# A SwiGLU FFN's first pair of column blocks by plain products in token halves instead of seven products, and its operand sums in place, on one Trainium2 core

## Chip, cores and metric

The kernel runs on one core of a Trainium2 chip. The metric is the device time of one execution in microseconds, lower is better.

## The reference

One layer over 1024 tokens of width 1024, all in float32. What matters here is its second half:

```python
x = layer_norm(DEEPNORM_ALPHA * x + mix, ln1_g[l], ln1_b[l])      # mix: attention branches, gated, projected
gu = x @ w_ffn_in[l]                       # 1024 x 1024 by 1024 x 5632
g, u = jnp.split(gu, 2, axis=-1)           # 2816 columns each
ffn = (jax.nn.silu(g) * u) @ w_ffn_out[l]
x = layer_norm(DEEPNORM_ALPHA * x + ffn, ln2_g[l], ln2_b[l])
```

Ahead of it stand the input projection, two attention branches of eight heads each, their gates and the output projection `mix`.

## The kernel before

Every float32 operand is split in a high part (rounded, written by ScalarE's copy, L109) and a low part (the rest, by VectorE's subtraction, L110), and a product is three matmuls: high by high, high by low, low by high.

The FFN's up stage works on 22 pairs `f`: one block of 128 gate columns (the left weights, `wL`) and one of 128 up columns (the right weights, `wR`). A pair is a 2 by 2 block product: rows are the two halves of the tokens (LO: 0 to 511, HI: 512 to 1023, in the kernel's order), columns are gate and up, and the inner dimension is cut in two halves of four k-tiles. It is computed with seven block products P1 to P7 instead of eight, in the order of `pair_steps`: P1, P2, P6, P5, P7, P3, P4. Each product (`product`, L171) has 4 k-tiles x 3 = 12 matmuls of 128x128 by 128x512, so a pair has 84. P1 goes to the accumulator `sx`, P2 to `sy`, P6 and P7 and P4 add on to `sx`, P5 goes to `sz` and P3 adds to it. Between them ScalarE and VectorE move partial results to SBUF (L188, L184, L197, L201), apply Silu to the gate (L850, L855) and multiply by up (L852, L856).

The weights' sums for a pair are made by `prep_right` (four subtractions of 512 columns and two splits of 1024), a split by `prep_left` and one by `prep_last`. The sums of the tokens' operands are made once, by `x1_operands`, from the first LayerNorm's output: after four token tiles (`hf` 0) TensorE transposes them (L789), and x1A1 (the operands of P1 and P2) is split from PSUM, with a plain copy `x1raw`; after the last four (`hf` 1) the other half is transposed, and for each of four k-tiles one after the other VectorE and ScalarE make `s13` (L803 to L805), x1A22 (P4's operand, L807), `s24` (L809, L810), and the splits x1S63 (P6 and P3) and x1S57 (P5 and P7). P1 and P2 thus need only the first four token tiles, all others need the last.

The output projection before it (`half_k` 1) goes through eight token tiles: 24 matmuls of the projection, VectorE's addition (L912), and the LayerNorm (L764 to L776; for the last two tiles of each half the end is VectorE's L771). The weights of pairs 0 to 2 are loaded and prepared around that loop.

`run_pairs` sets the order of the text: P1 and P2 of the first three pairs (`first=3`), then the rest of pair 0, the right weights of pair 1 after its first product, and so on. The order in which each engine's queue gets its instructions isn't that of the text: a scheduler at build time simulates the kernel and takes, for each engine, the first instruction in the text whose inputs and slots it believes ready. On the chip each queue is then worked in that fixed order. In the trace transposes (L789) stand between the matmuls of P1 and P2 (L171), for instance.

SBUF is handed out in slots of 128 x 1024 by tag (bw 9, pt 4, yt 3, gt 3, kp 4, op 8, xt 16, and the four tags of `QKV` with 2 each); PSUM in banks: mm 2, sc 2, tr 3, pv 1. A new tile waits until a slot of its tag is free. P1's accumulator takes "mm" (pair 2: "pv"), P2's and P5's "sc".

Of the kernel before, what the change touches and what calls it, by code (L numbers as in the profile page):

```python
# [12 lines left out]
F32R = mybir.dt.float32r  # L13
AF = mybir.ActivationFunctionType
ALU = mybir.AluOpType
# [32 lines left out]
def hybrid_trunk_kernel(ctx: ExitStack, tc, x, xt, w_in, b_gate, rel_bias, w_proj,  # L48
# [14 lines left out]
    def slot(tag, name, dtype=F32):  # L63
        return pool.tile([P, 1024], dtype, tag=tag, name=name, bufs=SLOTS[tag])
# [3 lines left out]
    def cycle(tags, name, dtype=F32):  # L68

        turn_of[tags] = turn_of.get(tags, -1) + 1  # L70
        return slot(tags[turn_of[tags] % len(tags)], name, dtype)
# [3 lines left out]
    def bank(tag, name):  # L75
        return ps.tile([P, HW], F32, tag=tag, name=name, bufs=BANKS[tag])
# [31 lines left out]
    def split(dst_h, dst_l, src):  # L108
        nc.scalar.copy(dst_h, src)  # L109
        nc.vector.tensor_tensor(dst_l, src, dst_h.bitcast(F32), ALU.subtract)  # L110

    def mm3(acc, pairs):
        n = len(pairs)
        i = 0
        for lh, ll, rh, rl in pairs:
            mm(acc, lh, rh, start=(i == 0), stop=False)  # L116
            mm(acc, lh, rl, start=False, stop=False)  # L117
            i += 1
            mm(acc, ll, rh, start=False, stop=(i == n))  # L119
# [8 lines left out]
    def prep_left(W, nm, src, tag="op"):  # L128
        L = W["L"] = slot("gt", f"wL{nm}")
        dma(L, src)  # L130
        W["hl"] = split_w(L, f"wl{nm}", tag)

    def split_w(raw, nm, tag):
        h = slot(tag, f"{nm}h", F32R)
        l = slot(tag, f"{nm}l", F32R)
        split(h, l, raw)
        return h, l

    def prep_right(W, nm, src, tag, tag_a=None):
        sub = ALU.subtract  # L140
        L = W["L"]
        R = W["R"] = slot("gt", f"wR{nm}")
        dma(R, src)
        ta = slot("kp", f"ta{nm}")
        tb = slot("kp", f"tb{nm}")
        nc.vector.tensor_tensor(ta[:, LO], R[:, LO], L[:, LO], sub)
        nc.vector.tensor_tensor(tb[:, LO], R[:, HI], ta[:, LO], sub)
        nc.vector.tensor_tensor(tb[:, HI], L[:, HI], tb[:, LO], sub)
        W["hb"] = split_w(tb, f"wb{nm}", tag)
        nc.vector.tensor_tensor(ta[:, HI], R[:, HI], R[:, LO], sub)  # L150
        W["ha"] = split_w(ta, f"wa{nm}", tag_a or tag)

    def prep_last(W, nm, tag):

        c = slot(tag, f"wc{nm}", F32R)
        split(c[:, LO], c[:, HI], W["R"][:, HI])
        W["c"] = c
# [216 lines left out]

        return pair_steps(f"p{i}", Wa[i], ops_x, c, done)

    def run_pairs(steps, left, right, also=lambda i: None, first=2, aside=lambda i: None):

        n = len(steps)
        for j in range(first):  # L380
            steps[j][0]()
            steps[j][1]()
        for i in range(n):
            rest = steps[i][2:] if i < first else steps[i]
            for j, p in enumerate(rest):
                p()
                if j == 0 and i + 1 < n:
                    right(i + 1)
                if j == 1 and i + 2 < n:
                    left(i + 2)  # L390
                aside(i)
            also(i)
# [384 lines left out]
            done(slice(0, D))  # L777

    ops_1 = {p: [] for p in range(1, 8)}
    x1raw = []  # L780

    def x1_operands(hf, acc_t):

        for kt in range(4):
            tps = []
            for k in (kt, kt + 4):
                tp = bank("tr", f"x1ps{hf}_{k}")
                for j in range(4):
                    tr(tp[:, j * P:(j + 1) * P], acc_t[4 * hf + j][:, k * P:(k + 1) * P], ident)  # L789
                tps.append(tp)  # L790
            if hf == 0:
                raw = slot("op", f"x1raw{kt}")
                for i in range(2):
                    o = slot("xt", f"x1A1{i}_{kt}", F32R)
                    split(o[:, LO], o[:, HI], tps[i])
                    nc.scalar.copy(raw[:, (LO, HI)[i]], tps[i])
                    ops_1[1 + i].append((o[:, LO], o[:, HI]))
                x1raw.append(raw)
            else:
                raw = x1raw[kt]  # L800
                s13 = slot("kp", f"x1s13_{kt}")
                s24 = slot("kp", f"x1s24_{kt}")
                nc.scalar.copy(s13[:, LO], tps[1])  # L803
                nc.vector.tensor_tensor(s13[:, HI], raw[:, LO], tps[0], ALU.subtract)
                nc.vector.tensor_tensor(s13[:, LO], tps[0], s13[:, LO], ALU.add)  # L805
                o = slot("bw", f"x1A22_{kt}", F32R)
                split(o[:, LO], o[:, HI], tps[1])  # L807
                ops_1[4].append((o[:, LO], o[:, HI]))
                nc.vector.tensor_tensor(s24[:, LO], s13[:, LO], raw[:, LO], ALU.subtract)  # L809
                nc.vector.tensor_tensor(s24[:, HI], raw[:, HI], s24[:, LO], ALU.subtract)  # L810
                for src, pa, pb, tags in ((s24, 6, 3, ("xt",)), (s13, 5, 7, QKV)):
                    h = cycle(tags, f"x1S{pa}{pb}h_{kt}", F32R)
                    l = cycle(tags, f"x1S{pa}{pb}l_{kt}", F32R)
                    split(h, l, src)
                    ops_1[pa].append((h[:, LO], l[:, LO]))
                    ops_1[pb].append((h[:, HI], l[:, HI]))

    for tt in range(8):
        dma(acc_t[tt], x[tt * P:(tt + 1) * P, :])
# [3 lines left out]

    Wf = [dict() for _ in range(NF)]
    def left_f(f):
        prep_left(Wf[f], f"f{f}", w_ffn_in[f], "pt" if f == 2 else "op")

    def right_f(f):
        prep_right(Wf[f], f"f{f}", w_ffn_in[NF + f], ("bw", "pt")[f % 2],
                   "op" if f == 1 else None)  # L830
        if f:
            prep_last(Wf[f], f"f{f}", "op")

    def up_steps(f):

        tl = {}

        def c(name):

            if name == "12":  # L840
                if "h" not in tl:
                    tl["h"] = cycle(("yt", "yt", "yt", "bw"), f"h{f}")
                return tl["h"][:, LO]
            if "t" not in tl:
                tl["t"] = slot(("yt", "yt", "bw")[f] if f < 3 else "kp", f"gt{f}")
            return tl["t"][:, LO if name == "11" else HI]

        def done(name, acc):
            if name == "11":
                nc.scalar.activation(c("11"), c("11"), AF.Silu)  # L850
            elif name == "12":
                nc.vector.tensor_tensor(c("12"), c("12"), c("11"), ALU.mult)  # L852
            elif name == "21":
                h = tl["h"]
                nc.scalar.activation(h[:, HI], acc, AF.Silu)  # L855
                nc.vector.tensor_tensor(h[:, HI], h[:, HI], c("22"), ALU.mult)  # L856
                if f in pair_of:
                    h_tiles[f] = h
                    if f % 2:
                        pieces.extend(left_sums(f - 1))  # L860
                else:
                    dma(h_dr[f], h)

        return pair_steps(f"f{f}", Wf[f], ops_1, c, done, "pv" if f == 2 else "mm")
# [34 lines left out]
    for half_k in range(2):  # L899
        wo = [load_w(w_out[(4 * half_k + j) * P:(4 * half_k + j + 1) * P, :], f"o{half_k}_{j}",  # L900
                     of("gt"), of("xt"), nc.vector) for j in range(4)]
        if half_k == 1:
            left_f(0)
            right_f(0)
            left_f(1)
        for tt in range(8):
            ts_ = slice(tt * P, (tt + 1) * P)
            for hf, cs in enumerate((LO, HI)):
                acc = bank("mm" if hf == 0 else "sc", f"ops{half_k}_{tt}_{hf}")
                mm3(acc, [(mh[4 * half_k + j][:, ts_], ml[4 * half_k + j][:, ts_],  # L910
                           wo[j][0][:, cs], wo[j][1][:, cs]) for j in range(4)])
                nc.vector.scalar_tensor_tensor(  # L912
                    acc_t[tt][:, cs], acc_t[tt][:, cs], ALPHA if half_k == 0 else 1.0, acc,
                    ALU.mult, ALU.add)
            if half_k == 1:
                layer_norm(acc_t[tt], g1, b1, f"1_{tt}", tt % 4 >= 2)
                dma(x1_dr[tt], acc_t[tt])
                if tt % 4 == 3:
                    x1_operands(tt // 4, acc_t)
                if tt == 3:  # L920
                    left_f(2)

    prep_last(Wf[0], "f0", "op")
    run_pairs([up_steps(f) for f in range(NF)], lambda f: left_f(f) if f > 2 else None, right_f,
              first=3, aside=next_piece)


    acc_t = [slot("op", f"x1_{tt}") for tt in range(8)]
# [154 lines left out]
```

## Time and profile before

| | us |
|---|---|
| median of 3 runs | 1477.51 (1477.05 to 1479.56) |
| the profiled execution's own time | 1477.29 |
| its span, first to last instruction | 1475.2 |
| TensorE (PE) busy | 1431.1 |
| VectorE (DVE) busy | 1040.6 |
| ScalarE (ACT) busy | 678.4 |
| GpSimd (POOL) busy | 279.6 |

In lines of the profile, `PE` is TensorE's matmuls and `PEld` its weight loads, which run beside them. `L171` is line 171 of the kernel. A timeline line has the start, the busy time, engine, line, operation, `output<-inputs` by the program's names without their numbers at the end, shapes and count; in brackets the idle time before it and what ended that. A line of waits has the waiting engine, line and tile, what it waited for, the total, the number of waits and the longest. Matmuls overlap in such lines: each shows 0.39 us, but the next starts before it ends.

### The profile page before, as it was taken

To read this page: it belongs to the slowest core of one execution; us is meant where nothing else is said; L and a number is where in the kernel's file an instruction comes from. 1 tells how busy PE (TensorE), PEld (TensorE's weight loads), DVE (VectorE), ACT (ScalarE), POOL (GpSimd) and SP (SyncE) were. 2 spreads that over 40 slices of the span, in tenths; PEclk is the share of its full clock that TensorE was granted. 3 is DMA by queue.
4 is the path that set the end of the run, shared out by engine and by line. 5 is a ranking of instruction groups with operands and counts; after the bars stand their busy time and mean duration, and the time that the engine had idled before them with its cause. 6 is when DMAs were issued, how large, how long until landed. Compare 5 with 4: busy or idle time off the path is not lost.

```text
span 1475.2 us, 19140 instructions
## 1 busy us (share of the span) xinstructions
PE 1431.1 (97%) x6728; PEld 1181.0 (80%) x6728; DVE 1040.6 (71%) x1698; ACT 678.4 (46%) x1176; POOL 279.6 (19%) x326
## 2 busy tenths in 40 slices
PE   8999999999999998999999799999999999999997
PEld 6788888887888787777888588888888888888886
DVE  7866555434776886887938966777766665978757
ACT  6444444334878878775403443444444443221201
POOL 0000000003555779760004100000000000100016
PEclk9999999999999999999999999999999999999999
DMA  6555545338667466757601133444444456887602
GB/s 214 157 187 172 160 147 183 124 95 235 195 196 202 123 212 194 227 181 258 211 15 72 58 114 114 155 145 155 145 154 147 145 196 240 316 293 249 214 15 100
DMA packets 83455, 247.72 MB, mean 168 GB/s; under 512 B 10512, under 2 KB 10512, under 8 KB 83360
## 3 DMA queue, kind: packets, MB, share of 16 engines
q1 hardware_dynamic: 83360, 246.51, 50.7%
q8 instruction: 53, 0.87, 0.2%
q14 instruction: 42, 0.34, 0.1%
HBM read 162.03 MB, written 80.77 MB: 165 GB/s over the span
## 4 chain that ended last, share of the span: by engine, by line
PE 85%; DVE 7%; DMA 3%; ACT 2%; issue 1%; POOL 1%; SPq 0%; POOLq 0%; DVEq 0%; ACTq 0%
PE sxf L171 16%; PE sxp L171 11%; PE szf L171 8%; PE dx L1016 6%; PE szp L171 6%; PE syf L171 4%; PE gps L419 3%; PE dz L1016 3%; PE syp L171 3%; PE yAps L619 2%; PE tp_b L559 2%; PE ops L117 2%; PE ops L119 2%; PE ops L116 2%; PE fpswh_h L116 1%; PE fpswh_h L117 1%
## 5 line engine op out<-in xcount | busy, mean ns | idle before, releaser
L972 POOL TENSOR_TENSOR wdyt<-wdyt 128x512 f32<-128x512 f32 x8 | 10.9, 1363 | 519.4 <-DVE wdgt L971 479.7
L536 POOL TENSOR_TENSOR w_b<-w_b,kp_b 128x511 f32<-128x511 f32 (+3 forms) x96 | 96.9, 1019 | 35.9 <-DVE kp_b L534 30.7
L534 DVE TENSOR_TENSOR_SCAN kp_b<-kp_b,ident_ps 128x384 f32<-128x384 f32 (+6 forms) x88 | 78.4, 891 | 7.0 <-ACT kp_b L526 2.2
L767 POOL TENSOR_TENSOR mv<-mv,neghalf 128x1 f32<-128x1 f32 x16 | 23.9, 1494 | 211.3 <-DVE mv L766 211.3
L480 POOL MEMSET bias<- 64x64 f32 x8 | 1.2, 144 | 330.0 <-ACT bias L479 330.0
L184 DVE TENSOR_TENSOR c<-sxp,c 128x512 f32<-128x512 f32 x16 | 11.1, 691 | 74.3 <-issue 41.2
L526 ACT ACTIVATE kp_b<-sc_b 128x512 f32<-128x512 f32 (+3 forms) x96 | 50.2, 523 | 23.8 <-PE sc_b L463 21.1
L110 DVE TENSOR_TENSOR pt_b<-tp_b,pt_b 128x512 fp32r<-128x512 f32 (+1 forms) x96 | 50.1, 540 | 12.5 <-ACT pt_b L109 12.2
L171 PE MATMUL szf<-x1S63h,wcf 128*128 128x512 f32 x176 | 57.8, 389 | 0.0
L947 DVE TENSOR_TENSOR x<-dx,x 128x512 f32<-128x512 f32 x64 | 43.5, 686 | 17.0 <-PE dx L1016 16.9
L110 DVE TENSOR_TENSOR sl<-h,sl 128x512 fp32r<-128x512 f32 x56 | 38.4, 685 | 20.6 <-ACT sl L109 20.6
L109 ACT CAST pt_b<-tp_b 128x512 fp32r<-128x512 f32 (+1 forms) x96 | 48.2, 515 | 8.2 <-PE tp_b L559 7.7
L501 POOL TENSOR_SCALAR w_a<-w_a,st_a 128x640 f32<-128x640 f32 (+2 forms) x64 | 42.7, 670 | 47.8 <-DVE st_a L500 32.8
L109 ACT CAST sl<-h 128x512 fp32r<-128x512 f32 x56 | 34.7, 619 | 37.0 <-PE syf L171 17.1
L559 PE MATMUL tp_b<-ident,w_b 128*128 128x128 f32 x288 | 47.9, 275 | 3.7 <-DVE pt_b L110 3.4
L110 DVE TENSOR_TENSOR pt_a<-tp_a,pt_a 128x512 fp32r<-128x512 f32 (+1 forms) x96 | 46.0, 486 | 7.7 <-ACT pt_a L109 6.6
L527 ACT ACTIVATE w_b<-sc_b 128x511 f32<-128x511 f32 (+3 forms) x96 | 50.4, 525 | 0.0
L116 PE MATMUL ops<-wh_o,mh 128*128 128x512 f32 x128 | 50.2, 392 | 0.0
L119 PE MATMUL ops<-wh_o,ml 128*128 128x512 f32 x128 | 50.0, 391 | 0.0
L117 PE MATMUL ops<-wl_o,mh 128*128 128x512 f32 x128 | 49.9, 390 | 0.0
L109 ACT CAST pt_a<-tp_a 128x512 fp32r<-128x512 f32 (+1 forms) x96 | 40.0, 425 | 20.3 <-PE tp_a L559 19.5
L855 ACT ACTIVATE h<-sxf 128x512 f32<-128x512 f32 x22 | 13.1, 597 | 76.8 <-PE sxf L171 76.8
(1887 smaller groups left out, 4828.2 us busy)
## 6 DMA issues: line engine op xcount, KB each, us to landing
s_dr<-sl SPq DMA_DIRECT2D x112, 256.0 KB, 2.3
sd<-s_dr SPq DMA_DIRECT2D x56, 512.0 KB, 4.5
wLf<-in_w_ffn_in_dram SPq DMA_DIRECT2D x22, 512.0 KB, 4.5
wRf<-in_w_ffn_in_dram SPq DMA_DIRECT2D x22, 512.0 KB, 3.6
wLp<-in_w_in_dram SPq DMA_DIRECT2D x17, 512.0 KB, 5.5
wRp<-in_w_in_dram SPq DMA_DIRECT2D x17, 512.0 KB, 4.1
v_dr<-v SPq DMA_DIRECT2D x16, 512.0 KB, 4.6
qs<-q_dr SPq DMA_DIRECT2D x16, 512.0 KB, 5.0
```

Of the source, the lines that this page charges most:

```text
L109: nc.scalar.copy(dst_h, src)
L110: nc.vector.tensor_tensor(dst_l, src, dst_h.bitcast(F32), ALU.subtract)
L116: mm(acc, lh, rh, start=(i == 0), stop=False)
L117: mm(acc, lh, rl, start=False, stop=False)
L119: mm(acc, ll, rh, start=False, stop=(i == n))
L171: mm(acc, lw[:, ks], rx, start=(first and kt == i == 0), stop=(kt == 3 and i == 2), skip_group_check=not first)
L526: nc.scalar.activation(kp[:, c0:e], sc[:, 0:n], AF.Sigmoid, scale=-1.0)
L527: nc.scalar.activation(be[:, m0:e], sc[:, m0 - c0:n], AF.Sigmoid)
L534: nc.vector.tensor_tensor_scan(kp[:, s0:e], kp[:, s0:e], ident_ps()[:, 0:e - s0], kp[:, s0 - 1:s0], ALU.mult, ALU.bypass)
L536: nc.gpsimd.tensor_tensor(be[:, m0:e], be[:, m0:e], kp[:, m0 - 1:e - 1], ALU.mult)
L559: tr(tp[:, (qb - lo_q) * P:(qb - lo_q + 1) * P], wt[qb - q0][:, (kb - qb) * P:(kb - qb + 1) * P], ident)
L1016: mm(acc, a, b, start=(first and i == n == 0), stop=(i == n - 1 == 1), skip_group_check=not first)
```

## The change

The first pair (`f` 0) is computed plainly: gate and up each by 8 k-tiles x 3 matmuls for the first token half and again for the second, 96 matmuls in all, without sums of its weights. Its first half stands in the text ahead of the other pairs, then P1 and P2 of pairs 1 and 2, then its second half, then the rest of pair 1 and on (`first=2`, and a new `then`). Pair 0's right weights are only split; pair 1's right weights are loaded and summed ahead of the projection's last loop, where pair 0's were. The second half of the plain pair needs x1A21, the split of a block that the seven products use only within sums: it takes four `QKV` slots.

`x1_operands` for `hf` 1 now first splits x1A21 and x1A22 and copies both to a tile `low`, for all four k-tiles, and then makes the sums in place in `low` and `x1raw`: all of x1S63 first, then all of x1S75. Four sums a k-tile, as before, but with both inputs in SBUF.

Slots: x1A22 goes from "bw" to "pt", pair 2's left weights from "pt" to "bw", the right weights of all pairs to "bw" (they took turns with "pt"). h and the gate of the plain pair take "yt".

```diff
     def run_pairs(..., first=2, aside=lambda i: None,
+                  then=lambda: None):
...
             steps[j][0]()
             steps[j][1]()
+        then()
...
     def x1_operands(hf, acc_t):
...
             else:
-                raw = x1raw[kt]
-                s13 = slot("kp", f"x1s13_{kt}")
-                s24 = slot("kp", f"x1s24_{kt}")
-                nc.scalar.copy(s13[:, LO], tps[1])
-                nc.vector.tensor_tensor(s13[:, HI], raw[:, LO], tps[0], ALU.subtract)
-                nc.vector.tensor_tensor(s13[:, LO], tps[0], s13[:, LO], ALU.add)
-                o = slot("bw", f"x1A22_{kt}", F32R)
-                split(o[:, LO], o[:, HI], tps[1])
-                ops_1[4].append((o[:, LO], o[:, HI]))
-                nc.vector.tensor_tensor(s24[:, LO], s13[:, LO], raw[:, LO], ALU.subtract)
-                nc.vector.tensor_tensor(s24[:, HI], raw[:, HI], s24[:, LO], ALU.subtract)
-                for src, pa, pb, tags in ((s24, 6, 3, ("xt",)), (s13, 5, 7, QKV)):
...
+                low = slot("kp", f"x1low{kt}")
+                for i, (o, to) in enumerate(((cycle(QKV, f"x1A21_{kt}", F32R), ops_21),
+                                             (slot("pt", f"x1A22_{kt}", F32R), ops_1[4]))):
+                    split(o[:, LO], o[:, HI], tps[i])
+                    nc.scalar.copy(low[:, (LO, HI)[i]], tps[i])
+                    to.append((o[:, LO], o[:, HI]))
+                x1low.append(low)
+        if hf == 0:
+            return
...
+        for kt in range(4):
+            raw, low = x1raw[kt], x1low[kt]
+            put(low[:, HI], low[:, LO], low[:, HI], ALU.add)
+            put(low[:, LO], raw[:, LO], low[:, LO], sub)
+            put(raw[:, LO], low[:, HI], raw[:, LO], sub)
+            put(raw[:, HI], raw[:, HI], raw[:, LO], sub)
+            split_two(raw, 6, 3, ("xt",), kt)
+        for kt in range(4):
+            split_two(x1low[kt], 7, 5, QKV, kt)
...
     def left_f(f):
-        prep_left(Wf[f], f"f{f}", w_ffn_in[f], "pt" if f == 2 else "op")
+        prep_left(Wf[f], f"f{f}", w_ffn_in[f], "bw" if f == 2 else "op")

     def right_f(f):
-        prep_right(Wf[f], f"f{f}", w_ffn_in[NF + f], ("bw", "pt")[f % 2],
-                   "op" if f == 1 else None)
-        if f:
+        prep_right(Wf[f], f"f{f}", w_ffn_in[NF + f], "bw")
+        if f > 1:
             prep_last(Wf[f], f"f{f}", "op")
+
+    def plain_half(half, x1):
+        accs = []
+        for key, tag in (("hl", "mm"), ("hr", "sc")):
+            accs.append(bank(tag, f"plain{key}_{half.start}f"))
+            wh, wl = Wf[0][key]
+            mm3(accs[-1], [(wh[:, k * P:(k + 1) * P], wl[:, k * P:(k + 1) * P], *x1[k])
+                           for k in (0, 4, 1, 5, 2, 6, 3, 7)])
+        nc.scalar.activation(gt0[:, half], accs[0], AF.Silu)
+        nc.vector.tensor_tensor(h0[:, half], accs[1], gt0[:, half], ALU.mult)
+
+    def plain_rest():
+        plain_half(HI, ops_21 + ops_1[4])
+        dma(h_dr[0], h0)
...
         if half_k == 1:
             left_f(0)
-            right_f(0)
+            R0 = slot("gt", "wRf0")
+            dma(R0, w_ffn_in[NF])
+            Wf[0]["hr"] = split_w(R0, "wrf0", "bw")
             left_f(1)
+            right_f(1)
...
-    prep_last(Wf[0], "f0", "op")
-    run_pairs([up_steps(f) for f in range(NF)], lambda f: left_f(f) if f > 2 else None, right_f,
-              first=3, aside=next_piece)
+    h0, gt0 = slot("yt", "h0"), slot("yt", "gt0")
+    plain_half(LO, ops_1[1] + ops_1[2])
+    prep_last(Wf[1], "f1", "op")
+    run_pairs([up_steps(f) for f in range(1, NF)], lambda i: left_f(i + 1) if i > 1 else None,
+              lambda i: right_f(i + 1), first=2, aside=next_piece, then=plain_rest)
```

More of the change, by code (lines that the diff above doesn't have):

```diff
@@ L375, in project, with run_pairs @@
         return pair_steps(f"p{i}", Wa[i], ops_x, c, done)
-    def run_pairs(steps, left, right, also=lambda i: None, first=2, aside=lambda i: None):
+    def run_pairs(steps, left, right, also=lambda i: None, first=2, aside=lambda i: None,
+                  then=lambda: None):
         n = len(steps)
@@ L779, in hybrid_trunk_kernel @@
     ops_1 = {p: [] for p in range(1, 8)}
-    x1raw = []
+    x1raw, x1low, ops_21 = [], [], []
     def x1_operands(hf, acc_t):
@@ L799, in x1_operands, with split_two @@
             else:
-                raw = x1raw[kt]
-                s13 = slot("kp", f"x1s13_{kt}")
-                s24 = slot("kp", f"x1s24_{kt}")
-                nc.scalar.copy(s13[:, LO], tps[1])
-                nc.vector.tensor_tensor(s13[:, HI], raw[:, LO], tps[0], ALU.subtract)
-                nc.vector.tensor_tensor(s13[:, LO], tps[0], s13[:, LO], ALU.add)
-                o = slot("bw", f"x1A22_{kt}", F32R)
-                split(o[:, LO], o[:, HI], tps[1])
-                ops_1[4].append((o[:, LO], o[:, HI]))
-                nc.vector.tensor_tensor(s24[:, LO], s13[:, LO], raw[:, LO], ALU.subtract)
-                nc.vector.tensor_tensor(s24[:, HI], raw[:, HI], s24[:, LO], ALU.subtract)
-                for src, pa, pb, tags in ((s24, 6, 3, ("xt",)), (s13, 5, 7, QKV)):
[L812 to L816, printed above, removed]
+                low = slot("kp", f"x1low{kt}")
[7 more added lines that the diff above has]
+            return
+        put, sub = nc.vector.tensor_tensor, ALU.subtract
+        def split_two(src, pa, pb, tags, kt):
+            h = cycle(tags, f"x1S{pa}{pb}h_{kt}", F32R)
+            l = cycle(tags, f"x1S{pa}{pb}l_{kt}", F32R)
+            split(h, l, src)
+            ops_1[pa].append((h[:, LO], l[:, LO]))
+            ops_1[pb].append((h[:, HI], l[:, HI]))
+        for kt in range(4):
[7 more added lines that the diff above has]
+            split_two(x1low[kt], 7, 5, QKV, kt)
     for tt in range(8):
```

## The prediction

> **What bounds the kernel now.** I read the page first: the engine totals and the shares of the chain that ended last.
>
> ```profile
> span 1475.2 us, 19140 instructions
> PE 1431.1 (97%) x6728; PEld 1181.0 (80%) x6728; DVE 1040.6 (71%) x1698; ACT 678.4 (46%) x1176; POOL 279.6 (19%) x326
> PE 85%; DVE 7%; DMA 3%; ACT 2%; issue 1%; POOL 1%; SPq 0%; POOLq 0%; DVEq 0%; ACTq 0%
> ```
>
> TensorE is the bound. So an edit here can do two things: change the number of matmuls, or change the time in which TensorE stands still. The change does both, in the stage between the output projection and the FFN's first pairs. Next the waits of TensorE from 815 us (last projection matmul) to 1249 us (end of the up stage).
>
> ```profile
> PE sxf L171 <- ACT x1S63h L109: 5.2, 2, 3.3
> PE x1ps L789 <- DVE acc L771: 1.9, 2, 1.1
> PE sxf L171 <- DVE x1S63l L110: 0.8, 1, 0.8
> ```
>
> All standing time of that long stage lies at two places: 1.9 us before transposes (L789), which wait for the last LayerNorms, and 6.0 us in f0's product P6 (accumulator sxf), which waits for its right operand x1S63. The timeline of TensorE shows where:
>
> ```profile
> 825.18 0.48 PE L171 MATMUL syf<-x1A,wlf0l 128*128 128x512 f32 x1
> ...
> 835.09 0.44 PE L171 MATMUL sxf<-x1S63h,wbf0h 128*128 128x512 f32 x1
> ...
> 838.62 0.50 PE L171 MATMUL sxf<-x1S63h,wbf0h 128*128 128x512 f32 x1 [1.93 <-ACT x1S63h L109]
> 839.88 0.50 PE L171 MATMUL sxf<-x1S63l,wbf0h 128*128 128x512 f32 x1 [0.76 <-DVE x1S63l L110]
> ...
> 843.89 0.79 PE L171 MATMUL sxf<-x1S63h,wbf0h 128*128 128x512 f32 x1 [3.28 <-ACT x1S63h L109]
> ...
> 849.20 0.39 PE L171 MATMUL szf<-x1S57h,waf0h 128*128 128x512 f32 x1
> ```
>
> From 849.20 on nothing waits. One window per stretch confirms it, and two short windows show the clock that TensorE was granted (the second to last column, a share of full speed):
>
> ```profile
> 815.00:835.09 20.09, 18.11 (x94) 14.11 (x92) 19.02 (x29) 9.46 (x14) 1.70 (x2) 1.00 0.17 70
> 835.09:849.20 14.11, 8.15 (x25) 5.73 (x25) 12.74 (x19) 8.30 (x11) 0.00 (x0) 0.76 0.13 38
> 849.20:1240.00 390.80, 390.80 (x1726) 323.60 (x1725) 265.04 (x359) 164.31 (x245) 0.00 (x0) 1.00 0.43 151
> ```
>
> ```profile
> 842.00:844.00 2.00, 0.11 (x1) 0.11 (x1) 2.00 (x5) 1.19 (x2) 0.00 (x0) 0.50 0.00 0
> 844.00:846.00 2.00, 2.00 (x5) 1.61 (x6) 1.70 (x2) 1.99 (x3) 0.00 (x0) 0.50 0.75 209
> ```
>
> The chain of waits, in order of time, gives the price of a product of 12 matmuls when nothing waits:
>
> ```profile
> 852.08 2.72 PE sxf L171 x12
> ```
>
> 2.72 / 12 = 0.2267 us a matmul. The stretch 835.09 to 849.20 holds two products, f0's P6 and f2's P2 (24 matmuls, 5.44 us), and lasts 14.11. So **8.67 us are lost** there: 1.93 + 0.76 + 3.28 = 5.97 standing, and 2.7 in matmuls spread out by half clock and late starts. The windows put the half clock behind the longest wait, granted 0.50 from 842 to 846.
>
> By the Trainium skill, page "TensorE: Matmul & The Clock Gate", Part 1, an idle window of about 3.4 us takes the array to half rate, and one busy window of that length brings it back. The rows agree: 0.50 right behind the 3.28 us wait.
>
> Why is x1S63 late? VectorE after the last LayerNorm:
>
> ```profile
> 820.75 1.41 DVE L771 SCALAR_TENSOR_TENSOR acc<-acc,mv,ln1b 128x512 f32<-128x512 f32 x2 [0.44 <-POOL mv L767]
> 822.08 0.68 DVE L804 TENSOR_TENSOR x1s<-x1raw,x1ps 128x512 f32<-128x512 f32 x1
> ...
> 824.49 0.68 DVE L809 TENSOR_TENSOR x1s<-x1s,x1raw 128x512 f32<-128x512 f32 x1
> 825.09 1.23 DVE L110 TENSOR_TENSOR x1S57l<-x1s,x1S57h 128x1024 fp32r<-128x1024 f32 x1
> 826.23 0.69 DVE L810 TENSOR_TENSOR x1s<-x1raw,x1s 128x512 f32<-128x512 f32 x1
> ...
> 843.28 0.68 DVE L184 TENSOR_TENSOR gt<-syf,gt 128x512 f32<-128x512 f32 x1
> 843.88 1.22 DVE L110 TENSOR_TENSOR x1S63l<-x1s,x1S63h 128x1024 fp32r<-128x1024 f32 x1
> ```
>
> From start to start, a sum of 512 columns takes 0.60 us (824.49 to 825.09) and a subtraction of 1024 columns 1.14 (825.09 to 826.23). Per k-tile the old code has four sums, the subtraction for x1A22 (0.60) and two of 1.14: 5.28, four times 21.1, from 822.08 to past 843. VectorE is full all that time. Note where the addition L184 stands: f0's P2 ended on TensorE with the row at 825.18, but its evacuation came at 843.28, behind the sums, as the scheduler goes by the order of the text among ready work.
>
> **The change part by part.**
>
> *Twelve matmuls more.* The first pair takes 2 sides x 2 halves x 8 k-tiles x 3 = 96 matmuls in place of 84. All sit on the bound engine: 12 x 0.2267 = **+2.72**. Page "TensorE: Matmul & The Clock Gate", section "Back-to-back issue gap", gives about 131 ns a matmul of 512 columns in a stream; by it the twelve would cost an estimated 1.57. The measured 0.2267 of this kernel decides.
>
> *More work in front of the first P6.* Before: P1 and P2 of three pairs, 72 matmuls. After: 48 (first half of the plain pair) + 48 (P1, P2 of f1 and f2) + 48 (second half) = 144. The first 96 need nothing of tokens 512 to 1023; the last 48 need only transposes and their splits. In the stretch 815.00 to 835.09 lie 60 of the matmuls, 13.60 us; the other 6.49 are the transposes and the 1.9 of waiting for LayerNorms, which I leave as they are, since the LayerNorm chain is not edited. TensorE then reaches the first P6 (now f1's) at 815.00 + 6.49 + 144 x 0.2267 = 854.1, if it never waits.
>
> *Are the operands there?* ScalarE's cadence on such tiles:
>
> ```profile
> 822.66 0.59 ACT L803 COPY x1s<-x1ps 128x512 f32<-128x512 f32 x1 [11.38 <-PE x1ps L789]
> 823.15 0.59 ACT L109 CAST x1A<-x1ps 128x512 fp32r<-128x512 f32 x1
> ...
> 842.79 1.04 ACT L109 CAST x1S63h<-x1s 128x1024 fp32r<-128x1024 f32 x1 [3.03 <-DVE x1s L810]
> 843.85 1.28 ACT L850 ACT_TABLE_LOAD   x1
> ```
>
> ScalarE: 8 casts and 8 copies at 0.49 (822.66 to 823.15) are 7.8, so x1A21 and x1A22 are done near 831, against the second plain half, due at 815.00 + 6.49 + 96 x 0.2267 = 843.3. VectorE: 8 subtractions of 0.60 (4.8), 16 sums (9.6), four of 1.14 for x1S63 (4.6): 19.0 us, from 822.7 to 841.7, and about 1 more for the last cast (1.04): 842.7. Were the sums to start only when ScalarE's 16 operations are over (830.5), it would be 830.5 + 14.2 + 1 = 845.7. Both lie before 854.1, by 8 to 11 us: **the 8.67 us go**. P5 and P7 need x1S75. Its first two tiles follow by about 848. The last two take slots that x1A21 holds until the second half's last product, so they come about 1.04 + 1.22 behind its last reads, near 856; P5 starts at 854.1 + 2.72 = 856.8, and its fourth k-tile 9 matmuls later.
>
> *Banks and slots.* The first half's accumulators fill one "mm" and one "sc" bank, f1 takes the others, f2's P1 has "pv". So 84 matmuls, until 815.00 + 6.49 + 19.04 = 840.5, need no evacuation. Then f2's P2 needs an "sc" bank, which VectorE frees by the multiplication into h0 or f1's addition. As L184 shows, such work comes behind the sums: 841.7 + 2 x 1.14 for the first x1S75 tiles = 844.0, + 0.6 = 844.6. But the second half's gate product needs only the "mm" bank, which ScalarE frees by the Silu, and TensorE can take its 24 matmuls first, until 846.0. That is the cover, 1.4 us deep; without it f2's P2 waits 844.6 - 840.5 = 4.1. Silu needs h0's and gt0's slots, those of LayerNorm tiles 4 to 6, free after the transposes near 830, and the table load of 1.28, which moves from 843.85 to there: ScalarE was busy 9.46 of 20.09 us in that stretch.
>
> *Weights.* f0's sums go (four of 0.60), its right columns are only split; f1's sums take their place before the loop. Net one cast and one subtraction of 1.14, when the projection's first half frees its slots. VectorE has room there:
>
> ```profile
> 772.77 0.69 DVE L912 SCALAR_TENSOR_TENSOR acc<-acc,ops 128x512 f32<-128x512 f32 x1 [1.30 <-PE ops L119]
> ...
> 778.21 0.69 DVE L912 SCALAR_TENSOR_TENSOR acc<-acc,ops 128x512 f32<-128x512 f32 x1 [1.07 <-PE ops L119]
> ```
>
> The gaps shown hold 2.37 us against 1.14: nothing, or 1.14 at most where they don't, as the LayerNorms would end later. On the DMA queue of SyncE, f1's right columns come before the loop; they no longer wait for f0's last split (issued at 843 before). The "bw" slots: 2 + 4 + 2 + 1 = 9 are full until f2's P2 frees two and the second half two more; f2's four weight tiles there have 60 matmuls (13.6 us) from then. Nothing on the path.
>
> *Sum:* -8.67 + 2.72 = **-5.95**, then the other pairs and the down stage as before. The span becomes 1469.25; the profiled execution, 1477.29 with 2.09 around its span, becomes 1471.3. It lies 0.22 under the median of 1477.51, so the time is **1471.6**.
>
> **The rivals.** What a run can tell from no change is about 0.2%, 2.95 us.
>
> A: *the wait moves to the bank.* f2's P2 is queued ahead of the second half's gate product and TensorE stands at 840.5 until VectorE frees "sc": 4.1 us, plus at most the 2.7 that the old wait cost beyond its standing time. Net -5.95 + 4.1 to 6.8 = -1.9 to +0.9: 1475.6 to 1478.4, no change. For it: the order of the text, and L184 at 843.28. Against: in the trace the scheduler did queue f0's P6 ahead of f2's P2, whose bank was not free; it looks for work that is ready.
>
> B: *slower: the same place, VectorE later still.* If the multiplication into h0 is queued behind x1S75's last tiles or f2's weight sums, while P2 stands first on TensorE, the wait and what it drags behind it pass 8.9 us. The point from which it decides: 840.5 + 5.95 + 2.95 - 2.7 = 846.7; an evacuation at 850 gives -5.95 + 9.5 + 2.7 = +6.2, 1483.8. For it: VectorE is full from 822 on, and my upper bound for the sums plus x1S75 is 848. Against: the second half itself needs that bank, and x1S75's last tiles need the second half, so they can't all stand in front.
>
> C: *more gain.* The 1.9 us before the transposes vanish too, if more of the first half's matmuls are queued in front of them: -7.8, 1469.7. For it: 96 matmuls instead of 72 are ready by then. Against: the same matmuls of f0 to f2 were ready in the trace, and the transposes were still queued first.
>
> D: *the change does little of what it says:* x1S63 is still late by some us. It would have to be 8 us later than worked out; with half of the old loss kept, -1.6, 1475.9.
>
> **How the numbers follow.** Forecast 0.67 (small waits of up to 2 us at the bank included, to 1473.6), C 0.08, A 0.10, D 0.05, B 0.10. Faster: forecast and C, 0.75; within 0.2%: A and D, 0.15; slower: B, 0.10. The range runs from 1469.2 (C, less 0.5 of spread among runs) to 1477.0, the middle of A; it leaves out B and half of A, under 2 in 10.
>
> **What would show it.** Right: 6740 matmuls in the page; no wait of sxf for x1S63 in TensorE's waits; granted clock 1.00 from 835 to 860; the first P6 near 854 and the up stage ending near 1243; L771 still ahead of transposes with about 1.9 us. The step that I trust least is the bank: a wait of syf or of the plain accumulators for VectorE at 840 to 846 shows A or B, and then the queue of VectorE there says which. The prediction is wrong if TensorE waits over 3 us in all between 822 and 870, or if a new wait shows in the pairs behind it.

## The result, and the profile after

The kernel with the change takes 1468.06 us, median of 5 runs (1465.8 to 1470.79), against 1477.51 before (1476.44 to 1479.56): a ratio of 0.9943, 95% interval 0.9922 to 0.9964. The medians differ by 9.45 us, the ratio alone would make it 8.4; 5.95 was forecast, and the range ended at 1469.2. The interval, 5.3 to 11.5 us, is too wide to settle a size of 6 or 8 us. The profile isn't, as it can be read by stage.

The profiled execution took 1466.33 us, its span is 1464.5. Its page, engine totals and chain:

```profile
span 1464.5 us, 19170 instructions
PE 1429.5 (98%) x6740; PEld 1181.3 (81%) x6740; DVE 1035.9 (71%) x1693; ACT 679.2 (46%) x1179; POOL 278.8 (19%) x326
PE 83%; DVE 7%; DMA 4%; ACT 2%; issue 2%; POOL 1%; SPq 0%; POOLq 0%; DVEq 0%; ACTq 0%
```

Twelve matmuls more, and yet TensorE's busy time is no longer; the half clock (granted 0.50), which had stretched some of them, is gone. "The projection's end" is from here on the start of the first transpose behind its last matmul: 815.00 before, 812.07 after. TensorE's waits of the kernel after, from there to 1239 (the end of the up stage), are one line, where there were three:

```profile
PE x1ps L791 <- DVE acc L773: 0.4, 1, 0.4
```

The timeline of TensorE in the kernel after, cut to the points at which the stage can be measured:

```profile
812.07 1.14 PE L791 MATMUL x1ps<-ident,acc 128*128 128x128 f32 x9
812.97 0.47 PE L116 MATMUL plainhl_0f<-x1A,wlf0h 128*128 128x512 f32 x1
...
835.52 0.39 PE L116 MATMUL plainhl_512f<-x1A,wlf0h 128*128 128x512 f32 x1
...
839.60 0.61 PE L171 MATMUL syf<-x1A,wlf2h 128*128 128x512 f32 x2
...
849.12 0.39 PE L171 MATMUL sxf<-x1S63h,wbf1h 128*128 128x512 f32 x1
...
851.84 0.39 PE L171 MATMUL szf<-x1S75h,waf1h 128*128 128x512 f32 x1
```

The row of 835.52 stands ahead of f2's P2 (839.60): TensorE's queue takes 18 of the 24 matmuls of the second half's gate product first. The windows of the stage:

```profile
812.07:849.12 37.05, 36.67 (x177) 30.07 (x176) 35.10 (x51) 24.25 (x36) 1.45 (x1) 1.00 0.20 71
849.12:1230.00 380.88, 380.88 (x1681) 315.08 (x1680) 254.91 (x345) 157.46 (x235) 0.00 (x0) 1.00 0.42 150
```

The granted clock is 1.00 in both. The first matmul of the down stage, where the up stage ends, starts at 1249.04 before and 1238.17 after. So the difference of the spans splits in this way:

| part of the execution | before | after | difference |
|---|---|---|---|
| start to the projection's end | 815.00 | 812.07 | -2.93 |
| from there to the end of the up stage | 434.04 | 426.10 | -7.94 |
| from there to the end | 226.16 | 226.33 | +0.17 |

In the first part TensorE's queue holds the same instructions in the same order in both programs. The second part is the change: 7.94 us, 2.0 more than the 5.95 of the sum.

In the experiments below "the stage" is this second part, and its "head" is the stretch from the projection's end to the first P6: 20.09 us before and 37.05 after, where the prediction had 39.13.

### The profile page after: what moved, and what is told of

Same layout as the page of the kernel before. It is cut to its first block, busy times and chain, and to the rows that moved or that the text cites. A ratio compares the mean times of both kernels' runs of the same rounds, so it can differ in the third digit from the quotient of the medians.

```text
span 1464.5 us, 19170 instructions
## 1 busy us (share of the span) xinstructions
PE 1429.5 (98%) x6740; PEld 1181.3 (81%) x6740; DVE 1035.9 (71%) x1693; ACT 679.2 (46%) x1179; POOL 278.8 (19%) x326
## 4 chain that ended last, share of the span: by engine, by line
PE 83%; DVE 7%; DMA 4%; ACT 2%; issue 2%; POOL 1%; SPq 0%; POOLq 0%; DVEq 0%; ACTq 0%
PE sxf L171 15%; PE sxp L171 12%; PE szf L171 8%; PE szp L171 6%; PE dx L1049 6%; PE syf L171 4%; PE gps L421 3%; PE dz L1049 3%; PE syp L171 3%; PE ops L119 2%; PE ops L117 2%; PE ops L116 2%; PE yAps L621 2%; PE dy L1049 1%; PE tp_b L561 1%
## 5 line engine op out<-in xcount | busy, mean ns | idle before, releaser
L500 ACT ACTIVATE w_a<-w_a,st_a 128x640 f32<-128x640 f32 (+2 forms) x64 | 44.7, 698 | 7.4 <-DVE st_a L495 5.7
```

## The experiments

The theory (S) was that those 2.0 us come from the slots: pair 2's left weights left "pt" for "bw", and so their split left the LayerNorms. Rival P was that the plain pair's matmuls hide the LayerNorms; a further one was that the sums' new order brings gain of its own. All times are compared with runs of the kernel before on the same chip.

**1. The slots alone** (`e1_slots`), seven products and old sums:

```diff
-                o = slot("bw", f"x1A22_{kt}", F32R)
+                o = slot("pt", f"x1A22_{kt}", F32R)
...
-        prep_left(Wf[f], f"f{f}", w_ffn_in[f], "pt" if f == 2 else "op")
+        prep_left(Wf[f], f"f{f}", w_ffn_in[f], "bw" if f == 2 else "op")
...
-        prep_right(Wf[f], f"f{f}", w_ffn_in[NF + f], ("bw", "pt")[f % 2],
+        prep_right(Wf[f], f"f{f}", w_ffn_in[NF + f], "bw",
```

> The kernel before with the change's slots alone: x1A22 in pt, pair 2's left weights and all right weights in bw; seven products for all pairs, sums as before. Theory S (slots): in the kernel before, the split wlf2 stands at 803.3 us among the LayerNorms, as its pt slots are those of LayerNorm tiles 0 to 3; with bw slots it runs near 768, where VectorE has gaps. So the last LayerNorm ends about 2 us sooner after the projection's last matmul (before: 5.75 us from that matmul's end to the last L771; after: 3.7), TensorE's wait for the LayerNorms falls from 1.9 to about 0.4 us, the wait for x1S63 stays near 6 us, and the time falls by about 2 us, to 1475.5. Rival P (plain pair): the shorter wait comes from the first half's matmuls in front of the transposes; then the wait stays 1.9 us here and the time within 0.5 us of 1477.5.

TensorE's queue is the same as before from end to end. Its waits in this stage:

```profile
PE sxf L171 <- ACT x1S63h L109: 4.7, 2, 2.8
PE sxf L171 <- DVE x1S63l L110: 0.8, 1, 0.8
PE x1ps L789 <- DVE acc L771: 0.4, 1, 0.4
```

The wait for the LayerNorms fell from 1.9 to 0.4, and the last L771 starts 3.71 us behind the projection's end (817.09 - 813.38). The head is 18.06 instead of 20.09: -2.03. Of these 1.5 are the shorter wait; the rest is in the transposes around it. But the stage is only 1.13 shorter (432.91), as the stretch from P6 to P5 lasts 14.94 instead of 14.11. The waits for x1S63 are not the reason: the last of them ends 2.04 us sooner as well (840.23 - 813.38 against 843.89 - 815.00). The loss lies behind it, where the same 15 matmuls take 6.15 us instead of 5.31. Windows of half a microsecond show the clock there: granted 0.50 from 835.6 to 845.9 in this execution, 10.2 us, and from 840.9 to 847.8 in the one before, 6.8 us. The ratio is 0.9987 (0.9977 to 0.9996). So S holds for the head; the expected 2 us left out that the half clock can last longer.

**2. The slots and the sums in place, in order of need** (`e2_sums`), seven products: x1A21's splits left out, the rest of `x1_operands` as in the change.

> The first experiment plus the sums in place in the order of need, still seven products for all pairs (no x1A21). From the rows of the kernel after: after the last LayerNorm VectorE has 4 subtractions for x1A22 (2.4), 16 sums (9.6) and 4 subtractions for x1S63 (4.6), 16.6 us, and x1S75 (4.6) partly between; P6 of pair 0 is due 20.7 us after the projection's end, 17 after the LayerNorms. Theory: P6 waits 1 to 4 us instead of 6, the time is 1470 to 1473, so the in-place order by itself takes back a part of the 8.7 us and the plain pair the rest. Rival: the order of the sums does nothing without the plain pair (as 4.6 us of x1S75 come in between): no less than 1475.

1475.97 us, ratio 0.9993 (0.9981 to 1.0006): the expectation failed, the rival was right. The stage is 434.55, longer than with the old sums (432.91). TensorE's waits there:

```profile
PE sxf L171 <- ACT x1S63h L109: 3.6, 2, 2.7
PE sxf L171 <- DVE x1S63l L110: 2.8, 2, 1.5
PE sxf L171 <- ACT h L197: 0.7, 1, 0.7
PE x1ps L789 <- DVE acc L771: 0.4, 1, 0.4
```

VectorE's queue in this kernel shows why: the last tile's x1S63 (841.88) stands behind all four subtractions of x1S75 (835.00, 837.87 and two from 839.61 on), and starts 26.8 us behind the projection's end, as in the first experiment. The text has them the other way, but while ScalarE's cast for that tile is under way (from 839.72), x1S75 is ready, and the scheduler takes it first.

**3. The change with the old sums** (`e3_old_sums`): `x1_operands` k-tile by k-tile from PSUM as before, with x1A21's split added (in the kernel that ran, just ahead of x1A22's); plain pair and slots as in the change.

> The kernel after with the old sums: per k-tile from PSUM, x1S63 and x1S57 of one k-tile before the next, x1A21 split last in each k-tile; plain pair and slots as after. Theory: the plain pair's 72 added matmuls in front of the first P6 (16.3 us) cover the sums in either order, x1S63 of the last k-tile comes near 841 and is due at 849: within 1 us of the kernel after, TensorE's waits between 812 and 870 under 1 us. Rival: the order of need carries the gain; then P6 or P5 waits and the time is 3 us or more above the kernel after.

1469.32 us, ratio 0.9946 (0.9929 to 0.9963); the stage is 426.05, the change's 426.10. The only wait is again 0.4 us for L773. The sums in place and their order bring nothing here: the theory holds.

**4. The change once more** (`e4_again`).

> The kernel after once more, unchanged, for its size against the kernel before and a second profile. The profile of the change was 10.7 us shorter in span, of which 2.9 us lie before 721 us, where all engines work on the same instructions in the same order as before. Theory: these 2.9 us are the spread of single executions; the change is worth 5.95 (the wait less 12 matmuls) + 2.1 (LayerNorms and transposes) = 8.0 us, 1469.5. Rival: the first 721 us are faster for a reason of the program (its size or place): then the second profile shows them again at 720.7 us, and the difference is 10 us or more.

1468.98 us against 1477.57, ratio 0.9946 (0.9928 to 0.9963). Its stage is 426.15. The projection's first matmul came at 722.26, not 720.66. Over the ten profiles of this study it came between 720.66 and 726.02, behind the same instructions, while the change's stage repeats within 0.05 us. So the 2.9 us of the first part are the spread of single executions, and the change is worth 7.9 us in the stage. The kernel before has one profile; how long its half clock lasts can shift that: in the first experiment a longer one cost 0.8 us.

**5. The split put back** (`e5_late_wl2`), everything else as in the change:

```diff
-        prep_left(Wf[f], f"f{f}", w_ffn_in[f], "bw" if f == 2 else "op")
+        prep_left(Wf[f], f"f{f}", w_ffn_in[f], "pt" if f == 2 else "op")
...
-                                             (slot("pt", f"x1A22_{kt}", F32R), ops_1[4]))):
+                                             (slot("pt" if kt < 2 else "bw", f"x1A22_{kt}", F32R), ops_1[4]))):
...
-        prep_right(Wf[f], f"f{f}", w_ffn_in[NF + f], "bw")
+        prep_right(Wf[f], f"f{f}", w_ffn_in[NF + f], "bw", "pt" if f > 1 and f % 2 else None)
```

> The kernel after with pair 2's left weights back in pt (x1A22 of k-tiles 2 and 3 goes to bw instead, and for odd pairs from 3 on two right-weight tiles to pt). TensorE's queue is the same instruction for instruction; VectorE's differs in the place of wlf2's split, which is again behind the first half's x1A1 splits, among the LayerNorms. Theory S: the last L773 starts 5.7 us behind the projection's last matmul instead of 3.7, TensorE waits 1.9 instead of 0.4 us for the LayerNorms, and the stretch from the projection's last matmul to the first P6 grows from 37.1 to 39.1 us, the number of the prediction; from there to the end of the up stage nothing changes. The time is 2 us above the kernel after. Rival: the plain pair's matmuls hide the LayerNorms, so the stretch stays at 37.1.

Its waits of TensorE in the stage are again one line:

```profile
PE x1ps L791 <- DVE acc L773: 1.9, 2, 1.1
```

The head is 39.10 (39.13 was predicted for the change), the stage 428.06: 1.96 above the change and 5.98 below the kernel before. This is the program that the prediction had described, and it is worth what the sum said; that 5.98 meets 5.95 so closely is in part luck, as the half clock of the kernel before is that of one execution. Its time, 1468.07 against 1474.7 (ratio 0.9948, 0.9931 to 0.9964), can't tell 2 us from none; the stage can.

**6. Twelve matmuls less** (`e6_less12`). It leaves out half of the inner sum of the up columns of pair 0 for the second token half, so that part of the output isn't the reference's:

```diff
+            ks = (0, 1, 2, 3) if half == HI and key == "hr" else (0, 4, 1, 5, 2, 6, 3, 7)
...
-                           for k in (0, 4, 1, 5, 2, 6, 3, 7)])
+                           for k in ks])
```

> The kernel after with 12 matmuls left out: the up columns of the first pair's second token half get only four of the eight k-tiles, so that part of the output lacks half of its inner sum. Theory: the stage is bound by TensorE, the twelve cost 12 x 0.2267 = 2.72 us, and the stretch from the projection's last matmul to the end of the up stage falls from 426.1 to 423.4 us with no new wait. Rival: they stand in time in which x1S75 or another operand is awaited anyway; then a wait takes their place and the stretch falls by less than 1 us.

The stage is 423.43: 2.67 and 2.72 below the change's two profiles, where 12 x 0.2267 gives 2.72. No new wait shows. The ratio is 0.9927 (0.9912 to 0.9941).

**7. Seven products with part of the split on GpSimd** (`e7_gpsimd`), the first experiment with x1S57's subtraction moved:

```diff
-                    split(h, l, src)
+                    nc.scalar.copy(h, src)
+                    (nc.gpsimd if pa == 5 else nc.vector).tensor_tensor(
+                        l, src, h.bitcast(F32), ALU.subtract)
```

> Seven products for all pairs, the slots of the change, the old sums, and the four subtractions of x1S57's split on GpSimd, which is idle there, instead of VectorE: 4 x 1.14 us less in VectorE's chain ahead of x1S63's last tile. Theory: in the first experiment the stretch from the first P6 to P5 lasts 14.9 us for 24 matmuls (5.44), 9.5 us lost; with 4.6 us less of VectorE 4 to 5 us of it remain, so the stretch from the projection's end to the end of the up stage falls from 432.9 to 427 to 429 us: a shorter chain of sums is worth its length, without one more matmul. Rival: GpSimd's subtraction (2.4 us for 1024 columns in the gates' stage) is later than P5 needs it, or slows VectorE's sums beside it; then the stretch stays above 431 us.

The rival was right: 1477.8 against 1474.7, ratio 1.0017 (1.0008 to 1.0026), slower. The stage is 436.86, 3.95 above the first experiment. TensorE stands 8.2 us there instead of 5.9, most of it at two places that are new:

```profile
PE syf L171 <- DVE gt L184: 3.8, 1, 3.8
PE x1ps L789 <- DVE x1s L805: 3.2, 2, 1.9
```

The timelines of VectorE and of GpSimd in this kernel show the second half of that rival:

```profile
825.02 0.68 DVE L110 TENSOR_TENSOR x1A<-x1ps,x1A 128x512 fp32r<-128x512 f32 x1
825.62 1.22 DVE L815 TENSOR_TENSOR x1S63l<-x1s,x1S63h 128x1024 fp32r<-128x1024 f32 x1
826.75 2.89 DVE L809 TENSOR_TENSOR x1s<-x1s,x1raw 128x512 f32<-128x512 f32 x1
829.57 0.67 DVE L804 TENSOR_TENSOR x1s<-x1raw,x1ps 128x512 f32<-128x512 f32 x1
```

```profile
826.61 2.49 POOL L815 TENSOR_TENSOR x1S57l<-x1s,x1S57h 128x1024 fp32r<-128x1024 f32 x1 [2.66 <-ACT x1S57h L814]
```

The sum L809 with both inputs in SBUF takes 2.89 us instead of 0.68 and ends (829.64) 0.54 us behind GpSimd's subtraction (829.10). Each of the four subtractions on GpSimd met such a sum: 2.42, 2.89, 2.87 and 2.84 us instead of 0.68, 8.3 us more in all, for the 4.6 that VectorE was spared.

**8. The late split without a clash** (`e8_no_clash`): the fifth experiment, with the addition of ln1b for token tile 5 on VectorE.

```diff
-            nc.gpsimd.tensor_tensor(t, t, b, ALU.add)
+            (nc.vector if name == "1_5" else nc.gpsimd).tensor_tensor(t, t, b, ALU.add)
```

> The fifth experiment (wlf2's split late) with one LayerNorm step more on VectorE: the addition of ln1b for token tile 5, which GpSimd did. In the kernel before and in the fifth experiment the next tile's L768 or L770 (two inputs in SBUF) starts beside that GpSimd addition and takes 3.3 us instead of 1.28. Theory C: of the 2.05 us that the late split costs, the price is this clash, which the split brings about by delaying VectorE by about its own length; with the addition on VectorE (about 1.14 us more work there) L770 takes 1.28 again and the last L773 starts 5.76 - 2.05 + 1.14 = 4.9 us behind the projection's last matmul, or less where VectorE had idle time. Rival: the split's own length is the price and the long L770 only a symptom; then the chain gets longer by the addition, 6.9 us.

Here is VectorE's timeline at that place:

```profile
813.78 1.22 DVE L778 TENSOR_TENSOR acc<-acc,ln1b 128x1024 f32<-128x1024 f32 x1 [0.15 <-ACT acc L777]
814.92 0.20 DVE L767 BATCH_NORM_AGGREGATE mv<-bn 128x2 f32<-128x12 f32 x1
815.04 0.63 DVE L943 SCALAR_TENSOR_TENSOR acc<-acc,ops 128x512 f32<-128x512 f32 x1
815.59 0.15 DVE L768 TENSOR_SCALAR mv<-mv 128x1 f32<-128x1 f32 x1
815.65 1.27 DVE L770 SCALAR_TENSOR_TENSOR acc<-acc,mv,ln1g 128x1024 f32<-128x1024 f32 x1
```

L770 takes 1.27 again, and the last L773 starts 4.80 us behind the projection's end (822.25 - 817.45), where the theory said 4.9 and the rival 6.9. Although VectorE has 1.14 us more to do, its chain is 0.96 shorter. As the step moved, the scheduler also put the transposes elsewhere, so that the chain's 1.09 us over the change's cost TensorE nothing: it waits for nothing in this stage, which lasts 426.02. The time, 1468.12 against 1476.23 (ratio 0.9948, 0.9932 to 0.9965), is that of the change. So two other forms of the kernel, this and the third experiment, reach the change's stage, and no complete one goes below it by more than 0.1 us: what is left in the head are matmuls, transposes and at most 0.4 us of waiting.

## Why the prediction was wrong

Direction, mechanism and the two large terms were right; a term that the sum had left as it was, was not.

*The lost 8.67 us and the 2.72 us* held. The fifth experiment, in which wlf2's split stays where it was before, as the prediction had silently taken it, gives -5.98 for -5.95, and the sixth gives 2.67 to 2.72 for the 2.72 by itself. The 8.67 is the size of one execution: in the first experiment, with the same queue of TensorE, the same stretch loses 9.50. The prediction put the half clock behind the longest wait. It sets in at 840.9, inside that wait, and in the first experiment at 835.6, before the longest wait (2.79) has begun. By the Trainium skill's figure of 131 ns ("TensorE: Matmul & The Clock Gate", section "Back-to-back issue gap") the twelve would have been an estimated 1.57; the run decides for the row.

*The operands* were in time. In the timeline of VectorE in the kernel after:

```profile
767.85 1.22 DVE L110 TENSOR_TENSOR wlf2l<-wLf,wlf2h 128x1024 fp32r<-128x1024 f32 x1
...
808.59 1.28 DVE L770 SCALAR_TENSOR_TENSOR acc<-acc,mv,ln1g 128x1024 f32<-128x1024 f32 x1
...
815.78 1.41 DVE L773 SCALAR_TENSOR_TENSOR acc<-acc,mv,ln1b 128x512 f32<-128x512 f32 x2 [0.44 <-POOL mv L769]
...
838.72 0.68 DVE L856 TENSOR_TENSOR h<-plainhr_0f,gt 128x512 f32<-128x512 f32 x1
...
840.52 1.22 DVE L110 TENSOR_TENSOR x1S63l<-x1raw,x1S63h 128x1024 fp32r<-128x1024 f32 x1
```

The last x1S63 ends at 841.74 against a first P6 at 849.12: 7.4 us of cover, 1 under the lower bound of 8.4. The sums came 26.0 us behind the start of the last L773, where the prediction had 22.0 to 25.0, as two x1S75 subtractions, the multiplication into h0 and two other operations stand in between.

*The bank*, the step trusted least, held too, by 0.2 us. The multiplication into h0 ends at 839.40, 23.6 us behind the start of the last L773 (the prediction's 844.6 was 23.9 behind its 820.75). TensorE worked on the second half's gate product meanwhile, as weighed, and began f2's P2 at 839.60; without those 18 matmuls it would have stood from 835.52. Rivals A and B did not occur, nor D.

*The step that failed* is this sentence: "the other 6.49 are the transposes and the 1.9 of waiting for LayerNorms, which I leave as they are, since the LayerNorm chain is not edited". The chain's text is not edited, but its place in VectorE's queue is shared with wlf2's split. Before, that split waited for "pt" slots that LayerNorm tiles 0 to 3 held, and ran in the middle of the chain. These are rows of the kernel before, of VectorE and of GpSimd, that the prediction did not use:

```profile
803.31 1.22 DVE L110 TENSOR_TENSOR wlf2l<-wLf,wlf2h 128x1024 fp32r<-128x1024 f32 x1
...
811.52 3.32 DVE L768 SCALAR_TENSOR_TENSOR acc<-acc,mv,ln1g 128x1024 f32<-128x1024 f32 x1
```

```profile
811.36 2.40 POOL L776 TENSOR_TENSOR acc<-acc,ln1b 128x1024 f32<-128x1024 f32 x1 [1.26 <-ACT acc L775]
```

And GpSimd's addition for the same tile in the kernel after:

```profile
806.39 2.40 POOL L778 TENSOR_TENSOR acc<-acc,ln1b 128x1024 f32<-128x1024 f32 x1 [1.26 <-ACT acc L777]
```

With the split there, tile 5's L768 starts at 808.42, 6.6 us ahead of the projection's end; in the kernel after it starts at 803.44, 8.6 ahead. These 2.05 us are the split's 1.14 and, in part, tile 6's first addition and statistics, which the scheduler then puts in front of it. So GpSimd's addition for tile 5 starts 2.04 us later, just ahead of tile 6's L768, which then takes 3.32 us instead of 1.28. Tile 6's L768 itself starts 3.48 us ahead of the projection's end in both kernels (811.52 and 808.59): the whole shift is that one long operation. After the change the split stands at 767.85, where VectorE had gaps before, one of which (1.30 us) the prediction had counted for other work, and L770 takes 1.28. The start of the last L771 or L773 moves from 5.75 to 3.71 us behind the projection's end, and TensorE waits 0.4 us, not the about 1.9 that the prediction named as its sign. The prediction listed the slot's move ("2 + 4 + 2 + 1 = 9") and asked only whether slots would run out, not when the tile would now be made. The first experiment shows the 2.03 us of the head by the slots alone, the fifth takes 2.05 back, and the eighth shows that the price is the clash and not the split's own length.

Rival C had the right size, 1469.7 and -7.8, and the wrong reason: it let more matmuls stand in front of the transposes. They do not: the first nine transposes are still queued ahead of them, at 812.07, and 13 matmuls stand before the next ones, in both kernels. With the stage's 7.94 alone the time would be 1469.6, just inside the range. The remaining 1.5 us to the measured 9.45 lie within the spread of executions, so that part of the miss is chance; the range had allowed 0.5 for it, and that was too little for medians of three to five.

## What to carry to other kernels

A slot decides not only whether a tile fits but when it is made: where a tile changes its tag, look up who held the old slot until when, and move its whole preparation in the queue of each engine before the sum is made. A stage between two fixed matmuls can be compared to 0.1 us where whole executions spread by 5 to 8 (the change's stage: 426.10 and 426.15), so read a small change there, and take the spread of medians into the range. Look at the granted clock first: a stage with a stretch of half clock in it isn't fixed to 0.1 us. An idle engine is no free place for work if it reads SBUF beside VectorE's operations with two inputs in SBUF: in the seventh experiment the 4.6 us moved away cost 8.3.

## What the runs showed of the hardware

VectorE's operations with two inputs in SBUF that started 0.15 to 0.55 us behind a GpSimd operation of 2.4 to 2.5 us with inputs in SBUF took 2.4 to 3.3 us instead of 0.68 or 1.28 (L768 before, L770 in the fifth experiment at 3.33, L809 and L810 in the seventh at 2.42 to 2.89). Those of 1024 columns ended 1.08 us behind GpSimd's end, those of 512 columns about 0.55. The Trainium skill, page "SBUF — State Buffer", section "Who interferes with whom", says that a VectorE instruction with two SBUF inputs contends with a GpSimd instruction that reads SBUF, that the shared pair of ports is an exclusive lock, and that the order of issue decides who blocks. The rows agree, down to the end times. They show the other order too: in the kernel before, GpSimd's addition for tile 4 starts at 803.87, 0.56 us behind wlf2's split on VectorE, and takes 2.92 us instead of 2.40. In the seventh experiment L804, with one input in PSUM, kept its 0.68 beside GpSimd at 821.49, and GpSimd its 2.41.

In the stage, half clock came with the standing time for x1S63 and is absent where that is gone (granted 1.00 from 812.07 to 1230 in the kernel after). Its length was 6.8 us before and 10.2 in the first experiment, with the same queue of TensorE.

One and the same queue of instructions took between 720.66 and 726.02 us up to the projection in the ten profiles. Stretches of half clock at varying places are a part of it. Windows over the time ahead of the projection show one of 3.4 us in the change's profile (from 579), two in that of the kernel before (from 363 and 582), and 13.7 us in all in the third experiment's. They are not all of it: the eighth experiment, with 6.8 us of half clock, came last. The rest stays open.
